# A two-layer encoder on one core: weight splitting moved from ScalarE and VectorE to GpSimd transfers that cast and add

## The chip, the core and the metric

One core of a Trainium2 chip runs the whole program. The metric is the device time of one execution in microseconds (us), and lower is better. The engines have short names in what follows: PE (TensorE, the matmuls; PEld is its weight load), DVE (VectorE), ACT (ScalarE), POOL (GpSimd) and SP (SyncE, which here only issues transfers). Each engine works through its own instruction queue in order, and an instruction whose semaphore isn't there yet holds up everything behind it on that engine.

## The reference, cut to what matters

512 tokens of 1024 channels pass through two layers and a final RMSNorm. In each layer one projection of the normalised input feeds three branches: (A) differential attention with four heads, (B) a retention with four heads, (C) a pooling mixer. Each branch is gated, and one output projection adds the result to the residual stream.

```python
h = rmsnorm(x, norm_w)
proj = jnp.einsum('bsd,de->bse', h, w_in)            # 1024 -> 4608 columns
aq, ak, av, ag, bq, bk, bv, bg, cu, cg = jnp.split(proj, splits, axis=-1)
...
mixed = jnp.concatenate([o_a, o_b, o_c], axis=-1)    # 1536 columns
return x + jnp.einsum('bse,ed->bsd', mixed, w_out)
```

All data are float32.

## The kernel before, in words

**Split products.** TensorE multiplies in a rounded float32 (`F32R`). So every operand is kept as two parts, a rounded one and what the rounding left over, and a product is three matmuls (`mm3`, line 499): high by high, high by low, low by high.

**Granules.** The weights stream through the core in 97 granules of 512 KB: 128 partitions by 1024 float32. A granule is used by 24 matmuls of 512 columns. `emit_granule` (line 428) makes a granule in three steps: a transfer on SP's queue into `wraw` (two buffers), a rounding copy on ACT into `wh`, and a subtraction on DVE into `wl` (`split`, line 453). `wh` and `wl` have five slots each (`WBUFS`, line 25). A granule's slot comes free when PE has read the granule that is five places ahead of it. As `wraw` is separate from these slots, the transfer can run up to two granules ahead of the free slot, and only the copy and the subtraction come after it.

**Units.** A layer is a list of named units (`ORDERS`, line 32). `bv` and `av` (`values`, line 694) take four granules at once and pass over four token tiles with them; a gate, `cu`, `cg` or half of a `qk` takes one granule (`proj_T`, line 515). Output units begin with `o` (`out_half`, line 557) and take one to four. The last unit, `oPQRS1`, takes four. `take` (line 443) emits granules until five past the current position exist. Layer 0 begins with `first_values` (line 702), which runs granules 0 to 3 against the transposed input as both arrive; `START` (line 27) is its order.

**Order.** The program is recorded first and then ordered by a list scheduler (`schedule`, line 201), which gives each engine its fixed order from estimated durations (`cost`, line 304). What the scheduler believes is not what the chip does: where an instruction is late on the chip, its engine's queue waits.

**Other users of the queues.** On SP's queue lie also the loads of x, the tables, and in `headnorm` (line 538) two small transfers that bring a row of statistics to all partitions. On POOL's queue lie the power operations of `headnorm` and `square` (lines 549 and 473), some clears in `c_pool` (line 905), and at the very end three products (line 989).

[...]

Of the kernel before, what the change touches and what calls it, by code (L numbers as in the profile page):

```python
# [9 lines left out]
F32 = mybir.dt.float32  # L10
# [19 lines left out]
# Order in which the units of a layer are recorded. An output unit is named by the pairs of 128-row blocks of w_out that it takes  # L30
# (A: P Q, B: R S, C: T U) and its half of the columns.
# [4 lines left out]
ORDERS = [o.split() for o in ORDERS]  # L36
PAIRS = {"P": ("A", 0), "Q": ("A", 2), "R": ("B", 0), "S": ("B", 2), "T": ("C", 0), "U": ("C", 2)}

# how far the units of a kind are moved ahead
# [4 lines left out]
# The kernel body is recorded first, on tiles that have no place yet. A list scheduler then fixes the order in which  # L44
# every engine issues its instructions and the slot each tile takes, and the program is emitted in that order.
# [17 lines left out]
class View:  # L63
    """Part of a recorded tile: partitions p0..p1, free offsets idx, and the steps that lead to it."""
# [32 lines left out]
    def window(self, row, first, pattern):  # L97
        """DRAM only: elements of a row from first on, by an access pattern of its own."""
        return View(self.base, self.p0, self.p1, self.idx, self.steps + (("window", row, first, pattern),))

    def spread(self, n):
        """Every element n times, along a new last axis."""
        return View(self.base, self.p0, self.p1, np.repeat(self.idx[..., None], n, -1), self.steps + (("spread", n),))
# [47 lines left out]
class Recorder:  # L151
# [9 lines left out]
    def add(self, name, engine, method, args, kw):  # L161
# [4 lines left out]
        ins = [v for v in list(args[1:]) + [x for k, x in kw.items() if k != "accum_out"] if isinstance(v, View)]  # L166
# [34 lines left out]
    def schedule(self):  # L201
# [39 lines left out]
        def ready(op):  # L241
            """A PSUM bank serves one engine at a time."""
# [55 lines left out]
WARM = 16  # matmuls on zeros at the start  # L298
QUEUE = 8  # transfers under way in a queue
FINE = 2  # weight granules of the first columns that come in two parts  # L300
# [3 lines left out]
def cost(engine, method, args, kw):  # L304
    """What an instruction weighs for the list scheduler: until its result stands, and on its engine."""
# [3 lines left out]
    if engine == "PE":  # L309
# [6 lines left out]
        return t, t  # L316
    if engine == "SP":
# [33 lines left out]
def record(ins: dict, out: bass.AP):  # L351
    nc = Recorder()
    x_d = ins["x"][0]
    w_in, w_out = ins["w_in"], ins["w_out"]
# [46 lines left out]
    def g_cols(l, c):  # L401
        return [w_in[l, :, c:c + P].rearrange("(k p) c -> p k c", p=P)]

    def g_tok(l, c):
        return [w_in[l, g * 256:(g + 1) * 256, c:c + 512].rearrange("(k p) c -> p k c", p=P) for g in range(4)]

    def g_out(l, e0, half):
        return w_out[l, e0:e0 + 256, HALF[half]].rearrange("(k p) c -> p k c", p=P)

    def unit_granules(l, u):  # L410
        if u in ("bv", "av"):
            return g_tok(l, BV if u == "bv" else AV)
        kind, i = u[:-1], int(u[-1])
        if kind in ("bg", "ag", "cu", "cg"):
            return g_cols(l, {"bg": BG, "ag": AG, "cu": CU, "cg": CG}[kind] + i * P)
        if kind == "bqk":
            return g_cols(l, BQ + i * P) + g_cols(l, BK + i * P)
        if kind == "qk":
            return g_cols(l, AQ + i * P) + g_cols(l, AK + i * P)
        if kind[0] == "o":  # L420
            return [g_out(l, "PQRSTU".index(c) * 256, i) for c in kind[1:]]
        return []

    granules = [g for l in range(DEPTH) for u in ORDERS[l] for g in unit_granules(l, u)]
# [3 lines left out]
    def emit_granule(parts=1):  # L428
        src = granules[len(wt)]
        shp = [P, src.shape[1], src.shape[2]]  # L430
# [28 lines left out]
    def square(t, half, junk, part=None):  # L459
        """Mean square of token tile t: the share of one half of its columns, or of a quarter in the second half."""  # L460
# [14 lines left out]
    def scaled(t, wb, dst, half):  # L475
        """One half of the columns of the rmsnorm of token tile t."""
        c = HALF[half]
        nc.vector.scalar_tensor_tensor(dst[:, c], xt[t][half], stats[t][:, 2:3], wb[:, c], op0=ALU.mult, op1=ALU.mult)

    def transpose4(src, step=None):  # L480
        """Four 128-column blocks of src, each transposed, in one bank."""
# [22 lines left out]
    def mm_stacked(ps, qk, m, cols):  # L504
        """Full product of slot m's query columns with its keys: both query parts lie stacked on partitions."""
# [16 lines left out]
    def stack_halves(dst, slots, src, scale, dup):  # L522
        """Split the 64 rows of each half of src. Without dup the low part goes to the other partition half of
        the same slot; with dup both parts take a slot each, present on both partition halves."""
# [13 lines left out]
    def headnorm(ov, scale, g):  # L538
        """ov * scale * rsqrt(mean over partitions of ov^2 + eps) * g"""
# [17 lines left out]
    def out_half(ms, half, after=None, before_end=None):  # L557
        """before_end: the last token tile comes in two quarters of the columns, and this follows the first."""
# [555 lines left out]
```

## Time and profile before

| | us |
|---|---|
| median of 2 runs (lowest, highest) | 682.1 (682.0, 682.2) |
| span of the profiled execution, first to last instruction | 679.9 |
[...]
| busy: PE, DVE, ACT, POOL | 659.5, 500.7, 353.9, 30.3 |
| weight granules: number, mean ACT copy, mean DVE subtraction | 97, 1.04, 1.21 |
| bytes moved by SP's queue, share of the 16 transfer engines | 71.29 MB, 36.3% |

How to read it: a busy PE isn't PE at full speed, because a matmul's end is modelled and neighbours overlap. The distance between the starts of two matmuls in a dense stretch is the true price. A wait is put down to what came last before it by the profile.

### The profile page before, as it was taken

To read this page: it belongs to the slowest core of one execution; us is meant where nothing else is said; L and a number is where in the kernel's file an instruction comes from. 1 tells how busy PE (TensorE), PEld (TensorE's weight loads), DVE (VectorE), ACT (ScalarE), POOL (GpSimd) and SP (SyncE) were. 2 spreads that over 40 slices of the span, in tenths; PEclk is the share of its full clock that TensorE was granted. 3 is DMA by queue.
4 is the path that set the end of the run, shared out by engine and by line. 5 is a ranking of instruction groups with operands and counts; after the bars stand their busy time and mean duration, and the time that the engine had idled before them with its cause. 6 is when DMAs were issued, how large, how long until landed. Compare 5 with 4: busy or idle time off the path is not lost.

```text
span 679.9 us, 8912 instructions
## 1 busy us (share of the span) xinstructions
PE 659.5 (97%) x3171; PEld 541.1 (80%) x3171; DVE 500.7 (74%) x954; ACT 353.9 (52%) x701; POOL 30.3 (4%) x51
## 2 busy tenths in 40 slices
PE   9969999999999999999999999899999999999996
PEld 7757887878788888887888888688888887888785
DVE  5468987787787998976574779767568957887733
ACT  7525673434376866553443756344447765655321
POOL 0000000000000000001010000000000000000011
PEclk9979999999999999999999999999999999999999
DMA  9447444323326223243322423532342143224302
GB/s 325 147 127 186 139 115 117 110 94 78 90 50 181 77 91 105 69 115 91 115 63 78 139 64 88 131 118 71 95 122 65 50 150 97 71 92 90 99 31 94
DMA packets 85141, 71.86 MB, mean 106 GB/s; under 512 B 6004, under 2 KB 67604, under 8 KB 85096
## 3 DMA queue, kind: packets, MB, share of 16 engines
q1 hardware_dynamic: 85096, 71.29, 36.3%
q8 instruction: 25, 0.41, 0.2%
q14 instruction: 20, 0.16, 0.1%
HBM read 69.09 MB, written 2.18 MB: 105 GB/s over the span
## 4 chain that ended last, share of the span: by engine, by line
PE 78%; DMA 10%; DVE 6%; issue 2%; ACT 2%; SPq 1%; POOL 0%; POOLq 0%; DVEq 0%; ACTq 0%
PE pj L1051 64%; PE lg L1051 6%; PE ov L1051 4%; PE tp L1051 4%; DMA hn<-row 3%; DMA wide<-dd 2%; DVE qk L1051 1%; DMA row<-edge 1%; DVE soft L1051 1%; DMA wraw<-in_w_in 1%; DVE wl L1051 1%; DMA cols<-in_scales 1%; DMA T<-in_xT_w 1%; DMA x<-in_x 1%; ACT soft L1051 1%
## 5 line engine op out<-in xcount | busy, mean ns | idle before, releaser
L1051 PE MATMUL pj<-hh,wh 128*128 128x512 f32 x448 | 178.5, 400 | 7.9 <-ACT wh L1051 6.5
L1051 PE MATMUL pj<-hl,wh 128*128 128x512 f32 x448 | 177.5, 397 | 0.0
L1051 PE MATMUL pj<-hh,wl 128*128 128x512 f32 x448 | 176.9, 396 | 0.0
L1051 ACT CAST wh<-wraw 128x1024 fp32r<-128x1024 f32 (+1 forms) x97 | 100.8, 1039 | 106.9 <-PE pj L1051 75.8
L1051 DVE TENSOR_TENSOR wl<-wraw,wh 128x1024 fp32r<-128x1024 f32 (+1 forms) x97 | 117.3, 1210 | 29.7 <-ACT wh L1051 29.1
L1051 PEld LDWEIGHTS pj<-hh,wh 128*128 128x128 f32 x448 | 84.7, 189 | 27.1 <-ACT wh L1051 7.0
L1051 PEld LDWEIGHTS pj<-hh,wl 128*128 128x128 f32 x448 | 84.6, 189 | 18.6
L1051 PEld LDWEIGHTS pj<-hl,wh 128*128 128x128 f32 x448 | 84.7, 189 | 17.7
L1051 PE MATMUL pj<-wh,mAC 128*128 128x512 f32 (+1 forms) x264 | 87.5, 391 | 0.0
L1051 ACT ACTIVATE soft<-soft,sm 128x512 f32<-128x512 f32 x96 | 67.8, 718 | 33.9 <-DVE sm L1051 33.5
L1051 DVE TENSOR_TENSOR x<-x,pj 128x512 f32<-128x512 f32 (+1 forms) x65 | 43.6, 675 | 23.2 <-PE pj L1051 22.8
L1051 PEld LDWEIGHTS pj<-wh,mAC 128*128 128x128 f32 x264 | 49.0, 188 | 10.3
L1051 PE MATMUL lg<-qk 128*128 128x512 f32 (+1 forms) x192 | 51.4, 361 | 1.5 <-DVE soft L1051 1.5
L1051 PE MATMUL pj<-wl,mAC 128*128 128x512 f32 (+1 forms) x132 | 51.4, 389 | 0.0
L1051 POOL TENSOR_TENSOR st<-st,neghalf 128x4 f32<-128x4 f32 (+1 forms) x28 | 25.1, 896 | 477.3 <-DVE st L1051 379.2
L1051 DVE CUSTOM_DVE_ANT_0 soft<-lg,wide 128x512 f32<-128x512 f32 x64 | 43.3, 687 | 1.9 <-PE lg L1051 0.3
L1051 PE MATMUL pj<-wh,mB 128*128 128x512 f32 (+1 forms) x136 | 44.5, 383 | 0.0
L1051 PE MATMUL pj<-wh,hl 128*128 128x512 f32 x104 | 41.4, 398 | 0.0
L1051 PE MATMUL pj<-wh,hh 128*128 128x512 f32 x104 | 41.3, 398 | 0.0
L1051 PE MATMUL pj<-wl,hh 128*128 128x512 f32 x104 | 41.2, 396 | 0.0
L1051 PEld LDWEIGHTS lg<-qk 128*128 128x128 f32 x192 | 32.5, 188 | 9.6 <-DVE soft L1051 2.5
L1051 PE MATMUL ov<-T,vh 128*128 128x256 f32 x192 | 39.1, 284 | 0.4 <-DVE og L1051 0.3
(151 smaller groups left out, 949.7 us busy)
## 6 DMA issues: line engine op xcount, KB each, us to landing
wraw<-in_w_in SPq DMA_DIRECT2D x71, 512.0 KB, 4.6
wraw<-in_w_out SPq DMA_DIRECT2D x24, 512.0 KB, 4.1
hn<-row SPq DMA_DIRECT2D x16, 256.0 KB, 3.9
wide<-gd SPq DMA_DIRECT2D x8, 448.0 KB, 4.0
T<-in_xT_w SPq DMA_DIRECT2D x8, 258.0 KB, 4.1
x<-in_x SPq DMA_DIRECT2D x8, 256.0 KB, 5.0
wide<-dd SPq DMA_DIRECT2D x8, 256.0 KB, 4.8
out<-T SPq DMA_DIRECT2D x8, 256.0 KB, 2.1
```

Of the source, the lines that this page charges most:

```text
L1051: op.inst = getattr(getattr(tc.nc, name), method)(*[real(a) for a in op.args], **{k: real(v) for k, v in op.kw.items()})
```

## The change

Host side: all weights are laid out anew as an array `wg` with one row block per granule, [granule][128][1024], so that a partition's share of a granule is 4 KB in one piece. `w_in` and `w_out` are no longer inputs. The list of granules is the same, in the same order.

Granules 0 to 3 are made as before, only from `wg`. Each of the other 93 is made by

1. a transfer on POOL's queue from `wg` (float32) into `wh` (`F32R`), which rounds if the transfer casts,
2. ACT: `wl` = -`wh`,
3. a second transfer on POOL's queue that adds the same granule of `wg` onto `wl`.

`wraw` has no part in them. With the last granule goes a guard: 512 of its high columns are rounded once more on ACT, the difference is formed on DVE, and a million times the difference is added to the residual tile `x[0][0]`. The scheduler's `cost` gets an entry for transfers on POOL, and the recorder learns that an accumulating transfer reads its target.

```diff
+        at, (nk, nc_) = granules[len(wt)]
+        shp = [P, nk, nc_]
+        src = ins["wg"][at].rearrange("p (k c) -> p k c", k=nk)
+        if len(wt) >= 4:
+
+            hi = sb("wh", shp, WBUFS, F32R)
+            lo = sb("wl", shp, WBUFS, F32R)
+            nc.gpsimd.dma_start(hi, src)
+            nc.scalar.activation(lo, hi.bitcast(F32), AF.Copy, scale=-1.0)
+            nc.gpsimd.dma_start(lo, src, accum_op=ALU.add)
+            wt.append((hi, lo))
+            if len(wt) == len(granules):
+                again, left = sb("soft", [P, S], 4, F32R), soft()
+                nc.scalar.copy(again, hi[:, 0, :].bitcast(F32))
+                nc.vector.tensor_tensor(left, hi[:, 0, :].bitcast(F32), again.bitcast(F32), op=ALU.subtract)
+                nc.vector.scalar_tensor_tensor(xt[0][0], left, 1e6, xt[0][0], op0=ALU.mult, op1=ALU.add)
+            return
         raw = sb("wraw", shp, 2)
...
+    if engine == "POOL" and method == "dma_start":
+        return 5500, 1500
...
+        kw_ins = [args[0]] if "accum_op" in kw else []
...
+    wg = np.empty((len(weight_granules()), P, 1024), np.float32)
+    for g, (name, l, (r, c), (nk, n)) in zip(wg, weight_granules()):
+        g[:] = np.asarray(inputs[name])[l, r:r + nk * P, c:c + n].reshape(nk, P, n).transpose(1, 0, 2).reshape(P, 1024)
+    a["wg"] = wg
```

## Rows read from the trace of the kernel before

**Rows 1.** The page: span and busy time of each engine.

```profile
span 679.9 us, 8912 instructions
...
PE 659.5 (97%) x3171; PEld 541.1 (80%) x3171; DVE 500.7 (74%) x954; ACT 353.9 (52%) x701; POOL 30.3 (4%) x51
```

**Rows 2.** Groups by line, op and tile: count, busy us, mean ns, idle before.

```profile
L1051 DVE TENSOR_TENSOR wl<-wraw,wh 128x1024 fp32r<-128x1024 f32 (+1 forms) x97 | 117.3, 1210 | 29.7 <-ACT wh L1051 29.1
L1051 ACT CAST wh<-wraw 128x1024 fp32r<-128x1024 f32 (+1 forms) x97 | 100.8, 1039 | 106.9 <-PE pj L1051 75.8 <-DMA wraw<-in_w_in 28.9 <-issue 1.8
...
L1051 DVE TENSOR_TENSOR qk<-soft,qk 64x512 fp32r<-64x512 f32 x32 | 21.9, 685 | 3.1 <-ACT qk L1051 2.4
...
L1051 DVE CAST qk<-qk 64x1024 fp32r<-64x1024 f32 x24 | 16.5, 689 | 0.7
...
L1051 POOL TENSOR_TENSOR soft<-x,T 128x512 f32<-128x512 f32 x3 | 3.9, 1302 | 19.9 <-DVE x L1051 13.5 <-issue 6.4
```

**Rows 3.** The chain that ended last, a dense stretch: start us, us, what.

```profile
352.06 37.49 PE pj L1051 x161
```

**Rows 4.** Windows of the start: length, busy us of PE, PEld, DVE, ACT, POOL; clock, transfer share, GB/s.

```profile
10.00:20.00 10.00, 10.00 (x45) 8.13 (x44) 6.76 (x13) 7.63 (x15) 1.11 (x2) 1.00 1.05 390
...
27.00:33.00 6.00, 6.00 (x28) 4.83 (x27) 2.50 (x8) 2.39 (x5) 0.00 (x0) 1.00 0.00 0
33.00:40.00 7.00, 0.79 (x4) 0.32 (x2) 2.30 (x5) 0.77 (x1) 0.00 (x0) 0.76 0.35 112
40.00:50.00 10.00, 9.67 (x36) 7.81 (x37) 8.31 (x26) 3.63 (x5) 0.00 (x0) 0.83 0.46 131
```

**Rows 5.** Waits of SP's queue: for whom, us in total, times, longest.

```profile
SPq L1051 <- DVE wl L1051: 302.6, 77, 17.0
...
SPq L1051 <- DMA row<-edge: 7.8, 1, 7.8
```

**Rows 6.** Timeline of the start, SP: start us, us, what.

```profile
23.95 0.38 SPq L1051 DMA_DIRECT2D row<-edge  x1
32.24 0.34 SPq L1051 DMA_DIRECT2D rb<-row  x1
32.69 9.25 SPq L1051 DMA_DIRECT2D wraw<-in_w_in  x3
```

**Rows 7.** Timeline of the start, PE and DVE around the stop.

```profile
37.70 0.69 DVE L1051 TENSOR_TENSOR cos<-cos,rb 128x512 f32<-128x512 f32 x1 [7.48 <-DMA rb<-row]
...
40.33 0.80 PE L1051 MATMUL pj<-hh,wh 128*128 128x512 f32 x1 [6.54 <-ACT wh L1051]
```

**Rows 8.** Transfers into wraw, time from issue to landing.

```profile
DMA to landing us min/median/max: 2.9/4.3/6.5
```

**Rows 9.** Timeline of ACT's copies: the start, layer 1's first values, the end.

```profile
28.36 1.04 ACT L1051 CAST wh<-wraw 128x1024 fp32r<-128x1024 f32 x1
...
363.51 1.05 ACT L1051 CAST wh<-wraw 128x1024 fp32r<-128x1024 f32 x1 [0.85 <-PE pj L1051]
...
640.44 1.05 ACT L1051 CAST wh<-wraw 128x1024 fp32r<-128x1024 f32 x1 [4.28 <-PE pj L1051]
...
650.18 1.05 ACT L1051 CAST wh<-wraw 128x1024 fp32r<-128x1024 f32 x1
```

**Rows 10.** Timeline: last matmul of layer 1's first values; first evictions of the last unit.

```profile
366.98 0.40 PE L1051 MATMUL pj<-wl,hh 128*128 128x512 f32 x1
...
657.14 0.69 DVE L1051 TENSOR_TENSOR x<-x,pj 128x512 f32<-128x512 f32 x1 [3.11 <-PE pj L1051]
```

**Rows 11.** Two windows in which PE stood still in mid-run (columns as in rows 4).

```profile
100.00:120.00 20.00, 18.38 (x101) 15.48 (x100) 15.87 (x25) 7.98 (x13) 0.00 (x0) 1.00 0.47 120
...
420.00:440.00 20.00, 17.52 (x94) 14.05 (x92) 16.31 (x26) 9.85 (x22) 1.02 (x1) 1.00 0.46 97
```

**Rows 12.** Waits of ACT: for whom, us in total, times, longest.

```profile
ACT wh L1051 <- PE pj L1051: 75.8, 39, 7.4
```

**Rows 13.** The chain: the power operation of one headnorm (columns as in rows 3).

```profile
298.51 1.02 POOL st L1051
```

More of the change, by code (lines that the diff above doesn't have):

```diff
@@ L36, with weight_granules @@
 ORDERS = [o.split() for o in ORDERS]
+def weight_granules():
+    out = []
+    for l in range(DEPTH):
+        for u in ORDERS[l]:
+            if u in ("bv", "av"):
+                out += [("w_in", l, (256 * g, BV if u == "bv" else AV), (2, 512)) for g in range(4)]
+                continue
+            kind, i = u[:-1], int(u[-1])
+            if kind in ("bg", "ag", "cu", "cg"):
+                out.append(("w_in", l, (0, {"bg": BG, "ag": AG, "cu": CU, "cg": CG}[kind] + i * P), (8, P)))
+            elif kind in ("bqk", "qk"):
+                out += [("w_in", l, (0, c + i * P), (8, P)) for c in ((BQ, BK) if kind == "bqk" else (AQ, AK))]
+            elif kind[0] == "o":
+                out += [("w_out", l, ("PQRSTU".index(c) * 256, 512 * i), (2, 512)) for c in kind[1:]]
+    return out
 PAIRS = {"P": ("A", 0), "Q": ("A", 2), "R": ("B", 0), "S": ("B", 2), "T": ("C", 0), "U": ("C", 2)}
@@ L165, in add @@
         outs = [args[0]] + ([kw["accum_out"]] if "accum_out" in kw else [])
-        ins = [v for v in list(args[1:]) + [x for k, x in kw.items() if k != "accum_out"] if isinstance(v, View)]
+        kw_ins = [args[0]] if "accum_op" in kw else []
+        ins = [v for v in list(args[1:]) + [x for k, x in kw.items() if k != "accum_out"] + kw_ins if isinstance(v, View)]
         deps, bases = {}, []
@@ L353, in record @@
     x_d = ins["x"][0]
-    w_in, w_out = ins["w_in"], ins["w_out"]
     def sb(tag, shape, bufs=1, dt=F32, name=None):
@@ L398, in record @@
     ident = sb("ident", [P, P])
[L401 to L424, printed above, removed]
+    granules = [(i, shape) for i, (_, _, _, shape) in enumerate(weight_granules())]
     wt = []
@@ L428, in emit_granule @@
     def emit_granule(parts=1):
-        src = granules[len(wt)]
-        shp = [P, src.shape[1], src.shape[2]]
+        at, (nk, nc_) = granules[len(wt)]
[14 more added lines that the diff above has]
+            return
         raw = sb("wraw", shp, 2)
@@ L1089, in _arrays @@
 def _arrays(inputs):
-    plain = ("x", "norm_w", "w_in", "diff_lambda", "pool_w", "w_out", "rel_bias", "final_norm_w")
+    plain = ("x", "norm_w", "diff_lambda", "pool_w", "rel_bias", "final_norm_w")
     a = {n: np.ascontiguousarray(inputs[n]) for n in plain}
```

## The prediction

> **What bounds the kernel now.** I read the page's busy times first: PE is busy for 659.5 of 679.9 us, DVE for 74%, ACT for 52%, POOL for 4% [rows 1]. A busy PE may still be slow, so the next view is the chain of waits, for the true price of a matmul: a stretch without a gap has 161 matmuls in 37.49 us, 0.233 us each [rows 3]. A granule feeds 24 matmuls, 5.6 us, and 97 granules make 543 us. The kernel is bound by PE, and a change beside PE can win only PE's standstill, some 20 us of the span. It can lose far more, because weights that come late stop PE at once.
>
> Where PE stands still is read from the windows. From 33 to 40 us it worked 0.79 of 7 us [rows 4]. The timeline shows how that ends: PE starts again at 40.33 after 6.54 us of idleness, when a `wh` copy is done [rows 7]. That copy waited for its transfer, and the timeline of SP shows why the transfer was late: it lay in SP's queue behind `rb<-row`, which needed the row issued at 23.95 and went out at 32.24; only at 32.69 came the weights [rows 5, 6]. DVE, too, sat 7.48 us in front of `cos`, for the same `rb` [rows 7], with a weight subtraction queued behind it. Afterwards the granted clock is down to 0.83, and PE starts 36 matmuls in the 10 us from 40 to 50 [rows 4] where 43 would fit at 0.233 us. The other two standstills that matter are 1.6 us and 2.5 us in mid-run [rows 11], both while DVE is loaded to about 80%. The rest lies ahead of the first weights and behind the last matmul, and the change doesn't touch it.
>
> **The change, part by part.**
>
> *Removed from DVE:* 93 subtractions of 1.21 us [rows 2], 113 us of its 501. DVE isn't the bound, so this counts only where PE waits for it: at most the 4.1 us of the two mid-run windows [rows 11]. I take half, -2.0 (from 0 to -4.1).
>
> *Removed from SP:* 93 transfers. SP waited 302.6 us for subtractions to free `wraw` [rows 5], with rows and tables queued behind; I count this with the 2.0.
>
> *ACT:* a copy of 1.04 us becomes a negation of the same size; I take 1.04, so nothing. The copies waited 75.8 us for PE to free a slot [rows 12]; now POOL has that wait, and ACT waits for the first transfer instead.
>
> *Added to POOL:* 186 transfers. No row shows the issue of one by POOL. Bounds: SP's issue of 0.38 us [rows 6] below, POOL's 1.30 us for an operation on 128x512 [rows 2] as the nearest row on that engine. I take 1.3: 242 us, 36% of POOL. What lies behind them are the power operations of each headnorm and norm, and their rows follow them on the way back to PE [rows 13]. POOL's queue also stops at its head, on a slot as ACT did (up to 7.4 us [rows 12]) or on ACT's negation. Four headnorms lie on the chain; four issues of 1.3 are 5.2 us, partly covered by other matmuls. I take +2.0 (0 to four waits of 7.4, 30).
>
> *The start.* Granules 4 to 8 no longer stand behind `rb<-row` on SP nor behind `cos` on DVE. PE could go on through three product banks from 33 to 44 us, and `rb` was there at 37.7 [rows 7]. Gain: 6.5 us of idleness and 7 matmuls of 0.233 (1.6 us) that the low clock cost, -8.1. Against it stands traffic: from 10 to 20 us the transfer engines are full at 390 GB/s [rows 4], where 512 KB take 1.34 us, and about one and a half granules more now move in that time. +2.0. (Ends: 0 if `rb` or the weights come that much later, -8.1 if the traffic is hidden.)
>
> *The way of a granule.* Before, the raw data lay ready when a slot came free, and copy and subtraction took 1.04 + 1.21 = 2.3 us. Now both transfers come after the slot. Call the time from free slot to finished `wl` C. The first transfer: issue 1.3 and landing 4.3 (median; 2.9 to 6.5 [rows 8]). The negation: 1.04 and about 1.0 in ACT's queue (ACT is busy half the time; up to the longest wait, 7.4). The second transfer: issue 1.3, and a landing that no row shows. It reads its target too, so below stands the 2.9 of a plain one and above twice the longest, 13. I take 6.5, the longest plain one, because the bytes read double while the fixed part of the landing doesn't. C = 1.3 + 4.3 + 1.0 + 1.04 + 1.3 + 6.5 = 15.4 us (8 to 30 with all ends together).
>
> With five slots, PE works on four other granules while one is filled, 4 x 5.6 = 22.4 us. C of 15.4 is hidden there. It isn't hidden where four granules are used together and come free almost at once:
>
> - *Layer 1's first values.* A slot came free just before 363.5 [rows 9], and the last matmul of the unit starts at 366.98 [rows 10]. One granule is already there, 24 matmuls, so PE lasts to 367.2 + 5.6 = 372.8. The next one stands at 363.4 + 15.4 = 378.8: +6.0 (0 at C of 9.4 or less). Layer 0's first values run over the granules one after another, and both `av` units are woven into attention heads, whose matmuls cover the gap; I cost these at nothing. Without that cover each `av` would cost the same 6.0.
> - *The last unit.* Its fourth granule got its slot just before 650.2 [rows 9], and PE needs it 1.4 us before the end of the first tile (evicted at 657.14 [rows 10]), at 655.7. It now stands at 665.6. PE can work on the other three granules for three tiles in three banks, 54 matmuls from 651.5, 12.6 us, to 664.1: +1.5.
>
> *The guard* is one ACT copy and two DVE operations in front of a DVE that stands idle for 3.1 us there [rows 10]: 0. If it stopped DVE until that granule's first transfer lands (650.2 + 1.3 + 4.3 = 655.8), the eviction at 657.14 would still be in time.
>
> *Sum:* 679.9 - 2.0 + 2.0 - 8.1 + 2.0 + 6.0 + 1.5 = 681.3 us of span. The median stands 2.2 above the span now, so 683.5.
>
> [...]
>
> **The rivals.**
>
> *R1, weights too late.* C comes near or above 22.4 us. Then every dense stretch stops PE once in each granule. At C = 26 the cycle of five slots is (26 + 5.6)/5 = 6.3 us a granule against 5.6; over about half of the 93 granules that is 33 us, with 16.6 at layer 1's first values and 12.1 at the end: 683.5 - 7.5 + 61.7 = 738; at C = 21 the dense stretches still hold, and 11.2 and 7.1 make 694. For it: the second landing is unknown, and POOL's and ACT's queues each stop at their heads. Against it: C must be half as long again as my sum. It decides above C of 22.
>
> *R2, POOL or the transfers can't keep pace.* On average a granule is wanted every (650.18 - 28.36)/91 = 6.8 us [rows 9], in dense stretches every 5.6. POOL falls behind from 2.8 us an issue, the engines if the adding transfer occupies them for more than 5.6 - 1.34 = 4.3 us, over three times a copy. At 8 us for both transfers: 92 x 8 = 736, with 28 us ahead and 24 behind, 788 us of span, 790 as a median. [...]
>
> *R3, faster by over 2%.* All gains and no loss: 679.9 - 8.1 - 4.1 + 2.2 = 670. It needs C under 9.4 and free traffic, and even so hardly reaches 668.5, since PE's matmuls alone leave so little.
>
> *R4, the transfer only copies.* Then `wh` isn't rounded and the guard shows it in the output. Its instructions and bytes are the same, so its time is that of the case it falls in.
>
> **How the numbers follow.** Forecast (C between 8 and 19, pace kept): 0.53, with its own range 672 to 697. R1: 0.18. R2: 0.19. R3: 0.08, mostly just short of 2%. Something else: 0.02. Two per cent, 13.6 us, is about what a measurement of this kernel can tell from no change. Within 2%, to 695.7: the forecast without its slow end (0.50) and most of R3 (0.05), 0.55. Slower by over 2%: R1, R2 and that end, 0.40. Faster by over 2%: 0.05. The range reaches down to R3's 670 and up through R1's 738, and leaves out R2 and little more.
>
> **What the profile would show.** The start: PE works through from 33 to 40 us and the granted clock stays at 1. Layer 1's first values: PE idle for some 6 us behind them, waiting for `wl` from a transfer. Dense stretches: no PE wait on `wh` or `wl`; if there is one in each granule, R1 or R2 holds, and the gap between issue and landing tells them apart: long landings with an idle POOL are R1 or full engines, a POOL busy to over 80% is R2. DVE: 93 subtractions gone and about 390 us busy. POOL's power operations: where they start more than 2 us after their inputs, the +2.0 was too small. The forecast is wrong if POOL's issues cost more than 2.8 us, or if the adding transfer lands after more than 11 us.

## The result and the profile after

The changed kernel takes 755.3 us (754.4 to 756.1) against 682.1 before: a ratio of 1.107, 95% interval 1.103 to 1.111. It is 73 us slower, above the forecast (683.5) and above its whole range (670 to 738).

The page of after, which answers to [rows 1], with two DMA queues added. q0 carries the transfers that POOL issues, q1 those of SP:

```profile
span 754.3 us, 8990 instructions
...
PE 682.7 (91%) x3171; PEld 553.2 (73%) x3171; DVE 406.7 (54%) x864; ACT 354.9 (47%) x702; POOL 163.1 (22%) x235
...
q0 software_dynamic: 26496, 96.48, 58.5%
q1 hardware_dynamic: 16680, 23.05, 11.2%
```

DVE has lost 94 us of work, as planned, and nothing came of it. PE stands still for 71.6 us of the span, before for 20.4. The line to stop at is q0: POOL's transfers hold the 16 engines for 58.5% of the span, 441 us, or 4.8 us for each of 92 granules. (92 is right, and all of them are in the trace. The text ahead of the prediction counts 97 granules and 93 moved ones, but 97 is the number of copies: the list in the kernel has 96 granules, and one of the first four comes in two parts.) Before, SP's transfers, nearly all that there were, held them for 36.3%.

Where PE stood still, by the waits of PE (for whom, us in total, times, longest):

```profile
PE tp L1064 <- ACT hn L1064: 12.8, 4, 6.0
PE pj L1064 <- DVE soft L1064: 7.6, 1, 7.6
PE pj L1064 <- DMA wl<-in_wg: 6.4, 6, 1.7
PE pj L1064 <- DVE u L1064: 5.7, 1, 5.7
PE tp L1064 <- DVE soft L1064: 5.2, 3, 2.8
...
PE tp L1064 <- DMA soft<-dd: 4.9, 1, 4.9
```

Only 6.4 us are direct waits for a weight that POOL brings. Most of the others are waits for headnorms (`hn`), for the products with `rb` (`soft`, `u`), for a table (`dd`); one of 5.1 us, not shown, is for a softmax column, and what stands behind it stays open. Worked out from the starts of neighbouring matmuls in the trace, against the usual distance for their kind: gaps longer by over 1.5 us hold 10.0 us before and 57.1 after, shorter ones 5.7 and 16.9, and matmuls that are up to 0.2 us late, such as those at a granted clock of 0.50 behind a stop, 9.7 and 24.5. The differences, 47.1, 11.2 and 14.8 us, make the 73.

Traced back through the waits of the other engines, the waits for `hn`, for the products with `rb` and for `dd` end at a transfer on SP's queue. (The longest of the three for `tp<-DVE soft`, 2.8 us, ends at ACT, which stood in front of a negation until a first transfer had landed, 9 us after its issue.) Issues with KB each and the median time to landing:

```profile
wh<-in_wg POOLq DMA_DIRECT2D x92, 512.0 KB, 5.0
wl<-in_wg POOLq DMA_DIRECT2D x92, 512.0 KB, 6.8
hn<-row SPq DMA_DIRECT2D x16, 256.0 KB, 5.7
...
x<-in_x SPq DMA_DIRECT2D x8, 256.0 KB, 7.7
...
rb<-row SPq DMA_DIRECT2D x1, 256.0 KB, 8.3
...
row<-edge SPq DMA_DIRECT2D x1, 2.0 KB, 9.3
```

Before, `hn` landed after 3.9 us, `x` after 5.0, `rb` after 5.4, and SP waited 7.8 us for `row<-edge` [rows 5]. (The two medians for `hn` rest on the 6 and 4 of its 16 transfers for which the view gives a landing. By the semaphore updates with which the transfers report their end, all 16 counted, they are 4.2 and 5.1. `row<-edge` takes 8.3 to 11.5 us in kernels without the change as well, so its 9.3 is no sign of load.) A headnorm's row makes two steps, a store to DRAM (`row<-st`) and the load of `hn`, and the store is later by as much: median 1.9 us before and 3.1 after, over all 16. SP's waits for it, in the kernel before:

```profile
SPq L1051 <- DMA row<-st: 14.0, 10, 2.8
```

and in the changed one:

```profile
SPq L1064 <- DMA row<-st: 49.1, 16, 6.1
```

VectorE's wait for `hn` has grown with them. Before:

```profile
DVE og L1051 <- DMA hn<-row: 17.4, 10, 5.6
```

The waits of POOL, ACT and DVE in the changed kernel:

```profile
POOL wl L1064 <- ACT wl L1064: 200.1, 63, 8.6
...
ACT wl L1064 <- DMA wh<-in_wg: 50.8, 23, 8.1
DVE og L1064 <- DMA hn<-row: 49.3, 11, 8.8
```

The longest of PE's waits for `hn`, 6.0 us, ends at 702.56, and the chain that leads there has both steps (start us, us, what):

```profile
688.62 5.81 DMA row<-st
...
694.49 6.48 DMA hn<-row
```

The start, in the windows (columns as in [rows 4]); the last one answers to [rows 11]:

```profile
20.00:40.00 20.00, 19.02 (x80) 14.99 (x81) 9.39 (x28) 12.74 (x24) 4.64 (x7) 1.00 1.00 299
40.00:60.00 20.00, 11.71 (x45) 8.63 (x43) 6.71 (x28) 1.62 (x2) 2.88 (x4) 0.82 0.70 118
60.00:80.00 20.00, 10.07 (x30) 7.51 (x31) 7.36 (x14) 5.16 (x6) 3.40 (x8) 0.58 0.66 129
420.00:440.00 20.00, 17.11 (x73) 13.29 (x72) 3.19 (x5) 7.46 (x10) 5.24 (x7) 1.00 0.93 197
```

and the kernel before, in the third of them:

```profile
60.00:80.00 20.00, 20.00 (x90) 16.01 (x89) 16.34 (x22) 14.62 (x21) 0.06 (x2) 1.00 0.59 163
```

Until 40 us PE does better than before. Then it starts 45 and 30 matmuls in windows of 20 us where the kernel before started 79 and 90, and the granted clock is down to 0.82 and 0.58 of full speed. These are means: in windows of 1 us it is 1.00 from 30 to 52 us, 0.50 from 53 to 76 and 1.00 again from 77. Over the whole span it is 0.956, before 0.994. The timeline says why (start us, us, what, and the idle time before it), to be read beside [rows 6, 7]:

```profile
36.98 0.37 SPq L1064 DMA_DIRECT2D row<-edge  x1
46.33 0.34 SPq L1064 DMA_DIRECT2D rb<-row  x1
...
54.75 0.69 DVE L1064 TENSOR_TENSOR cos<-cos,rb 128x512 f32<-128x512 f32 x1 [12.67 <-DMA rb<-row]
...
56.81 0.63 ACT L1064 ACTIVATE gate<-soft 128x512 f32<-128x512 f32 x1 [15.81 <-DVE soft L1064]
...
61.78 1.04 ACT L1064 ACTIVATE wl<-wh 128x1024 fp32r<-128x1024 f32 x1
...
63.25 0.87 POOL L1064 DMA_DIRECT2D wl<-in_wg  x1 [18.93 <-DVE hn L1064]
...
56.83 0.80 PE L1064 MATMUL pj<-hh,wh 128*128 128x512 f32 x1 [7.62 <-DVE soft L1064]
```

`row<-edge` goes out 13 us later than before because `x` came late (ACT's last square on it starts at 34.54, before at 22.16), it takes 9.3 us, and `rb` lands at 54.7 in place of 37.7. Of these 17 us, then, 13 come from the late `x`. Four queues show what follows. DVE stands in front of `cos` for 12.7 us, and PE starts again at 56.83 after 7.6. ACT stands in front of `gate`, which needs a product with `rb`; behind `gate` in its queue lie an operation on a table, for which it waits 3.4 us more, and then a negation, done at 62.8. POOL stands 18.9 us in front of the transfer that adds to it. (The row names DVE's `hn`. The next such transfer, at 65.09, follows its negation by the same 0.4 us, so it was the negation.)

### The profile page after: what moved, and what is told of

Read it like the earlier page. It is cut to its first block, busy times and chain, and to the rows that moved or that the text cites. A ratio compares the mean times of both kernels' runs of the same rounds, so it can differ in the third digit from the quotient of the medians.

```text
span 754.3 us, 8990 instructions
## 1 busy us (share of the span) xinstructions
PE 682.7 (91%) x3171; PEld 553.2 (73%) x3171; DVE 406.7 (54%) x864; ACT 354.9 (47%) x702; POOL 163.1 (22%) x235
## 3 DMA queue, kind: packets, MB, share of 16 engines
q0 software_dynamic: 26496, 96.48, 58.5%
q1 hardware_dynamic: 16680, 23.05, 11.2%
## 4 chain that ended last, share of the span: by engine, by line
PE 44%; DMA 23%; issue 18%; POOL 6%; DVE 5%; ACT 3%; SPq 0%; POOLq 0%; DVEq 0%; ACTq 0%
PE pj L1064 37%; DMA hn<-row 5%; DMA row<-st 4%; PE lg L1064 4%; DMA wh<-in_wg 4%; POOL wl L1064 3%; DMA wl<-in_wg 2%; PE tp L1064 2%; POOL wh L1064 2%; DMA sin<-in_c_sin 2%; POOL st L1064 2%; PE ov L1064 1%; DMA wraw<-in_pool_w 1%; DVE soft L1064 1%; DMA row<-edge 1%
## 5 line engine op out<-in xcount | busy, mean ns | idle before, releaser
L1064 PE MATMUL pj<-hh,wh 128*128 128x512 f32 x448 | 181.1, 405 | 15.2 <-DVE soft L1064 7.6
L1064 PE MATMUL pj<-hh,wl 128*128 128x512 f32 x448 | 180.4, 405 | 4.7 <-DMA wl<-in_wg 4.7
L1064 PE MATMUL pj<-hl,wh 128*128 128x512 f32 x448 | 180.1, 403 | 0.0
L1064 POOL DMA_DIRECT2D wl<-in_wg x92 | 82.6, 898 | 231.4 <-ACT wl L1064 200.1
L1064 ACT ACTIVATE wl<-wh 128x1024 fp32r<-128x1024 f32 x92 | 96.7, 1056 | 53.3 <-DMA wh<-in_wg 50.8
L1064 PEld LDWEIGHTS pj<-hh,wh 128*128 128x128 f32 x448 | 86.5, 193 | 36.0 <-DVE soft L1064 8.3
L1064 POOL DMA_DIRECT2D wh<-in_wg x92 | 54.8, 595 | 251.0 <-PE pj L1064 248.4
L1064 PE MATMUL pj<-wh,mAC 128*128 128x512 f32 (+1 forms) x264 | 90.3, 405 | 3.7 <-ACT mAC L1064 3.0
L1064 DVE TENSOR_TENSOR x<-x,pj 128x512 f32<-128x512 f32 (+1 forms) x65 | 43.8, 675 | 37.8 <-PE pj L1064 37.6
L1064 PEld LDWEIGHTS pj<-wh,mAC 128*128 128x128 f32 x264 | 51.2, 197 | 15.6 <-ACT mAC L1064 3.4
L1064 PE MATMUL pj<-wl,mAC 128*128 128x512 f32 (+1 forms) x132 | 53.6, 406 | 0.0
```

Of the source, the lines that this page charges most:

```text
L1064: op.inst = getattr(getattr(tc.nc, name), method)(*[real(a) for a in op.args], **{k: real(v) for k, v in op.kw.items()})
```

## Experiments

One execution each where no interval is given; those of the kernel before lay between 680 and 685 us beside them, so that 5 us are no difference. Four theories of the 73 us stood at the beginning, and their names return in the expectations: **traffic** (the engines are so loaded that other transfers land late), **way** (a granule takes longer than the other four cover), **heads** (what stands behind a waiting instruction on POOL or ACT is late), **order** (the planner's new order is worse). In the diffs, `+` and `-` are against the changed kernel.

### The two halves, the layout, and fewer bytes

The layout alone:

```
-        if len(wt) >= 4:
+        if len(wt) >= 1000:
```

> The changed kernel with all 97 granules on the old path (SP's transfer, ACT's copy, VectorE's subtraction), but still read from the packed array in rows of 4 KB. Four theories of the 73 us lost are under test. Traffic: the two transfers of POOL hold the transfer engines for 58.5% of the span, so everything else that is moved (rows, x, tables, headnorm rows) lands later, and the stages behind it stop TensorE. Way: from a free slot to a finished wl it takes longer than the 22.4 us that the other four granules cover. Heads: POOL's and ACT's queues stand with their first instruction on a slot or a transfer, and what is queued behind it (power operations, copies) is late. Order: the planner's order of the work became worse with the new instructions. All four expect this kernel near the one before, 675 to 685 us, because none of what they blame is in it. A time above 690 would say that the packed layout itself costs something; under 675, that it helps.

682.2 us, ratio 0.999 (0.997 to 1.002): the packed array costs and gives nothing. It is the base of the later kernels on the old path.

Only the first transfer:

```
+            raw = sb("wraw", shp, 2)
 ...
+            nc.sync.dma_start(raw, src)
             nc.gpsimd.dma_start(hi, src)
-            nc.scalar.activation(lo, hi.bitcast(F32), AF.Copy, scale=-1.0)
-            nc.gpsimd.dma_start(lo, src, accum_op=ALU.add)
+            nc.vector.tensor_tensor(lo, raw, hi.bitcast(F32), op=ALU.subtract)
```

> Half of the change: POOL's transfer rounds into wh, the raw granule comes by SP as before, and VectorE subtracts wh from it; no adding transfer, no negation. The bytes moved are the same as with both halves, but the second transfer is a plain one. Traffic: if rounding and adding cost the engines alike, about 2.4 us each where a plain one costs 1.3 to 1.4, this gives back a quarter of the excess, 720 to 745; if the adding one is the costly one, 685 to 710. Way: issue, landing of 5.0 and a subtraction of 1.2 us are some 8 us, well covered, 680 to 695. Heads: POOL has half of its instructions and no wait for ACT, ACT none for a transfer, 690 to 720. Order: 680 to 690.

699.6 us. q0 on its page:

```profile
q0 software_dynamic: 13248, 48.24, 21.8%
```

Only the second:

```
+            raw = sb("wraw", shp, 2)
 ...
-            nc.gpsimd.dma_start(hi, src)
+            nc.sync.dma_start(raw, src)
+            nc.scalar.copy(hi, raw)
             nc.scalar.activation(lo, hi.bitcast(F32), AF.Copy, scale=-1.0)
             nc.gpsimd.dma_start(lo, src, accum_op=ALU.add)
```

> The other half: the raw granule comes by SP, ACT rounds it into wh and negates that into wl, and only the adding transfer is POOL's; no subtraction on VectorE. Traffic: as for the other half, 720 to 745 if both kinds cost alike; 730 to 755 if the adding one is the costly one. Way: 1.0 + 1.0 + 0.9 + 6.8 us and queues make some 11 us, covered: 680 to 695. Heads: POOL waits for ACT as before but not for slots, ACT has one more copy but waits for early transfers only, 695 to 725. Order: 685 to 695.

733.1 us. q0:

```profile
q0 software_dynamic: 13248, 48.24, 37.8%
```

The same number of packets and bytes on both pages, and not the same load: 21.8% of 697.8 us over 92 transfers is 1.65 us each, 37.8% of 731.3 is 3.0. The packets say it too: one of 4 KB takes 159 ns (median) when SP only copies it, 174 when it is rounded, 328 when it is added. By these medians rounding in flight is nearly free, and adding costs the engines twice a copy. The halves cost 17 and 51 us; each of them still carries SP's raw granules, which the whole change doesn't. An adding packet took 1.89 times as long as a rounding one (328 against 174 ns). That it reads its target too was my reason for a longer landing; no run here shows whether that read is what takes the time.

All instructions and waits, an eighth of the bytes:

```
+            fh, fl, fs = (v.rearrange("p k c -> p (k c)") for v in (hi, lo, src))
+            nc.vector.memset(fh[:, P:].bitcast(F32), 0.0)
-            nc.gpsimd.dma_start(hi, src)
+            nc.gpsimd.dma_start(fh[:, 0:P], fs[:, 0:P])
 ...
-            nc.gpsimd.dma_start(lo, src, accum_op=ALU.add)
+            nc.gpsimd.dma_start(fl[:, 0:P], fs[:, 0:P], accum_op=ALU.add)
```

> The changed kernel, but both transfers of POOL move only the first 128 of 1024 columns of each granule (an eighth of the bytes; VectorE fills the rest of wh with zeros, ACT's negation the rest of wl, so seven eighths of each weight granule are left out). All instructions, waits and slots stay. Traffic: the stolen time goes with the bytes, 685 to 700 us, and x, rb, row and hn land as before the change (4 to 5, 5.4, 3.1 and 3.9 us). Way: the landings of 5.0 and 6.8 us shrink by the part that the bytes make, at most some 2 us each, so the way falls from about 17 to 13 us or more; if the way is what stops TensorE, 690 to 720. Heads: POOL still waits 200 us and more for slots and for ACT, so at least 730. Order: no change, 745 to 755.

708.7 us: 46.6 of the 73 come back. q0 and the landings, columns as above:

```profile
q0 software_dynamic: 26496, 12.07, 12.2%
...
wh<-in_wg POOLq DMA_DIRECT2D x92, 64.0 KB, 2.2
wl<-in_wg POOLq DMA_DIRECT2D x92, 64.0 KB, 2.7
hn<-row SPq DMA_DIRECT2D x16, 256.0 KB, 3.8
...
rb<-row SPq DMA_DIRECT2D x1, 256.0 KB, 3.8
```

`hn` and `rb` land no later than before the change, and so VectorE's wait for the headnorms' rows, 49.3 us in the changed kernel, is small again:

```profile
DVE og L1066 <- DMA hn<-row: 10.3, 8, 2.4
```

The landings of POOL's own transfers fell as well, so this run alone doesn't tell traffic from way. About 26 us stay.

### Traffic, way or heads

Traffic that nobody waits for, beside the old path. The first form of it (878.4 us) missed its purpose: the planner put the transfers far ahead of their granules, and they filled the engines until 507 us.

```
 (old path for all granules)
+            nc.gpsimd.tensor_copy(mark, hi[:, 0, 0:1].bitcast(F32))
+            spare = nc.tile("dram", "spare", [P, 1040], 4, F32R)[:, 0:1024]
+            nc.gpsimd.dma_start(spare, ins["wg"][at])
+            nc.gpsimd.dma_start(spare, ins["wg"][at], accum_op=ALU.add)
```

> The old path for all granules (as with the packed layout alone, 682.2 us), and beside it, for each granule from the fifth on, the two transfers of POOL with their bytes (one rounding, one adding), into spare DRAM that nobody reads; POOL issues them when the granule's wh has been rounded. So the traffic is there and nothing waits for it. Traffic (what is lost is lost because rows, x, rb and headnorm rows land later): 46 of the 73 us came back when the bytes were taken away, so 715 to 735. Way and heads: only POOL's power operations stand behind the new issues, 682 to 692. If transfers into DRAM hold the engines for less than those into SBUF (1.65 and 3.0 us), the traffic theory's figure falls in that proportion.

The second form puts both transfers behind `mark` in the planner's order too:

```
+                nc.ops[-1].deps.append(m)
```

> As the last kernel with free traffic, but paced: there the planner had put POOL's transfers ahead of the granules they belong to, so they ran as fast as the engines allowed and filled them until 507 us. Here the two transfers into spare DRAM stand in POOL's order behind the copy that waits for the granule's own wh. Nothing waits for them. Traffic: 46 of the 73 us came back when the bytes were taken away, and DRAM targets cost the engines about as much as SBUF ones (4.42 against 4.65 us a granule), while SP's raw transfers, 1.4 us a granule, come on top: 720 to 750. Heads and way: 682 to 692.

809.6 us, 127 more than without these transfers, where 40 to 70 were expected. q0, and the landing of SP's raw granules (3.9 us with the layout alone):

```profile
q0 software_dynamic: 26496, 96.48, 51.9%
...
wraw<-in_wg SPq DMA_DIRECT2D x95, 512.0 KB, 7.1
```

Transfers whose data nobody uses cost more here than the whole change did. The size was missed because SP's raw granules now land late as well, and `wh` with them: ACT waits 81.6 us for them in 29 times. A part may not be traffic: POOL waits 226 us for its own spare tiles to come free, and its power operations stand behind that. So the run shows the direction, and the size is only a bound.

A sixth slot:

```
-WBUFS = 5
+WBUFS = 6
 ...
-        raw = sb("wraw", shp, 2)
+        raw = sb("mB", shp, 4)
 (the one other tile that lay in wraw moves to T)
```

> The changed kernel with six slots for weights in place of five (the first four raw granules lie in tiles that layer 0 doesn't use yet, so the memory is there). Transfers, bytes and instructions stay; a granule gets 5.6 us more of cover. Way: the waits for wl and all that follows from them go, 690 to 720. Traffic: the lateness of rows and tables stays, 740 to 755. Heads: POOL's heads wait as long as before in sum, but for slots further ahead, so what stands behind them is late as before: 735 to 755.

755.0 us, no difference. The headnorms' rows are as late:

```profile
DVE og L1064 <- DMA hn<-row: 45.7, 12, 8.0
```

So it isn't too few slots for the way of a granule. The second transfer copying in place of adding:

```
-            nc.gpsimd.dma_start(lo, src, accum_op=ALU.add)
+            nc.gpsimd.dma_start(lo, src)
```

> The changed kernel with the second transfer copying (and rounding) instead of adding, behind the same negation, so the low part of the weights is left out; instructions, order and waits stay. By the halves run alone, an adding transfer holds the engines for 3.0 us and a rounding one for 1.65, so the load falls from 4.65 to 3.3 us a granule. Traffic: about 45 us belong to 4.65 us a granule; with 3.3, 715 to 735. Way: the second landing falls from 6.8 to about 5.0 us, 1.8 of some 17 us, so at least 740. Heads: at least 740.

722.9 us, 32 less:

```profile
q0 software_dynamic: 26496, 96.48, 44.2%
```

44.2% of 721.0 us over 184 transfers is 1.73 us each. With order, instructions and bytes untouched, adding in place of copying is worth 32 of the 73 us. Two things go with it: the second transfer lands sooner (4.6 us for 6.8), and its issue on POOL is shorter (mean 0.56 us for 0.90). The sixth slot says that the first is worth little; the next run bears on the second.

POOL left to its transfers:

```
-            nc.gpsimd.tensor_tensor(st[:, 2:3], st[:, 1:2], neghalf[:, 0:1], op=ALU.pow)
+            nc.vector.tensor_scalar(st[:, 2:3], st[:, 1:2], 0.0, 1.0, op0=ALU.mult, op1=ALU.add)
 ...
-            nc.gpsimd.memset(u[:, 0:PADL], 0.0)
+            nc.vector.memset(u[:, 0:PADL], 0.0)
 (the headnorms' power operation and the other border of u in the same way)
```

> The changed kernel with POOL left to its transfers (and the last three products): the clearing of u's borders goes to VectorE, and the power operations are replaced by a VectorE operation of the same tiles that writes 1.0, so the norms' factors are left out. Heads: what stood behind POOL's waits (u's borders at 63 us, the 28 power operations) comes in time, which is the part that taking the bytes away didn't give back, some 26 us: 720 to 735. Traffic and way: the transfers and slots are as before, 745 to 755, less at most 5 for the power operations' own time on the way of 16 headnorms.

748.9 us: 6.4 less, little above what one run can tell; the expectation had laid POOL's 18.9 us at the start to u's borders, and they were ACT's. What stands behind POOL's waits is a small part.

### The start and the plan

The first 12 granules on the old path:

```
-        if len(wt) >= 4:
+        if len(wt) >= 12:
```

> The changed kernel, but the first 12 granules keep the old path, so the start is that of the kernel before and POOL's transfers begin some 40 us later. The start of the changed kernel lost about 18 of the 73 us (309 matmuls by 80 us before, 220 after). Traffic that delays x and rb at the start is a part of the loss of its own: 735 to 742. If the same loss is only moved to where POOL's transfers begin: 750 to 756.

732.2 us: 23 us belong to the start, more than the 13 to 20 that the range expected.

The planner told what transfers take in the changed kernel:

```
     if engine == "POOL" and method == "dma_start":
-        return 5500, 1500
+        return (6800, 900) if "accum_op" in kw else (5000, 600)
 ...
                 op.end = bus + 908
+                to, of = (v.base.tag if isinstance(v, View) else "" for v in op.args[:2])
+                op.end += 7300 if (to, of) == ("row", "edge") else 5600 if to == "rb" else 2500
```

> The changed kernel whole; only the planner's costs are set to what the changed kernel's transfers took: first transfer 5.0 us (0.6 of POOL), second 6.8 (0.9), row<-edge 7.3 more than assumed, rb 5.6 more, every other transfer of SP 2.5 more. Bytes and instructions are the same. Stale plan (the order was laid out for transfers that land earlier, and TensorE stands where it meets them): most of the 73 us comes back, 690 to 715. Capacity (the transfers are slow by themselves and no order hides them): 735 to 755.

721.7 us with every byte and every instruction of the change: 33.5 us back, between the two expectations. POOL's transfers land as late as before this edit (5.3 and 6.9 us), SP's a little sooner (`rb` 6.4 for 8.3 us, `x` 5.4 for 7.7, `hn` over all 16 rows 4.5 for 5.1). So the new order moves the work that needs them further back, and it also moves the transfers themselves; this run doesn't part the two. Two of PE's waits, the longest in total and that for weights:

```profile
PE tp L1066 <- ACT hn L1066: 7.0, 6, 2.3
...
PE pj L1066 <- DMA wl<-in_wg: 3.2, 4, 1.2
```

Either way, nearly half of the loss goes with an order made for transfers that land earlier than they did. Both edits together, told costs and 12 granules on the old path:

> The planner told the measured landings (721.7 us alone) and the first 12 granules on the old path (732.2 us alone). The two edits gave back 33.5 and 23.0 us; were they independent, 698.7. If both mend the same thing at the start (with the told costs the matmuls by 100 us are 375 against 315 in the changed kernel, so part of the start is mended there already), 708 to 722. What is left above 682 is then what the engines' load costs with an order that fits it.

725.4 us, above both expectations and no better than the told costs alone: the two gains don't add. Not because the start was already whole. By 100 us this kernel has started 415 matmuls, with the told costs alone 371; by 600 us they stand at 2664 and 2665. The lead from the start is lost on the way, and why is open. (The told costs are those of the loaded engines, and with the old path the start isn't loaded so.)

Only the headnorms' rows late, and no traffic; the planner is kept from knowing:

```
 (old path for all granules; in the planner, the step out of hop ends when it starts)
-        nc.sync.dma_start(row.rearrange("(p j) -> p j", j=4), st[:, 4:8])
+        nc.sync.dma_start(hop.rearrange("(p j) -> p j", j=4), st[:, 4:8])
+        nc.sync.dma_start(row, hop)
```

> No part of the change: the old path for all granules, but each of the 16 headnorms' rows takes one more step through DRAM (2 KB from one row to another) that the planner is not told of, so hn comes some 2 to 4 us later without any traffic. In the changed kernel row and hn together come about 2 to 5 us later than before. If late headnorm rows alone are what stops TensorE in mid-run: 715 to 730 (some 50 us over 16 headnorms, 3 us each). If they are mostly covered: 684 to 695, and the loss needs the lateness of the weights and the other transfers as well.

700.9 us, 18.7 above the old path with the same layout, for a step that lands after 2.2 us, 16 times. DVE's wait, before 17.4 us:

```profile
DVE og L1067 <- DMA hn<-row: 30.2, 13, 4.4
```

Over half of 35 us of lateness reaches the end. This is less than the mid-run loss, but it needs no late weight at all.

### Two versions of the old path, and what remains

The same correction of the planner's costs without the change. First the start alone, then all transfers (the second edit has 900 in place of 0):

```
 (old path for all granules)
                 op.end = bus + 908
+                to, of = (v.base.tag if isinstance(v, View) else "" for v in op.args[:2])
+                op.end += 6000 if (to, of) == ("row", "edge") else 2700 if to == "rb" else 0
```

> No part of the change: the old path for all granules from the packed layout, with one correction in the planner's costs, that row<-edge lands 6.0 us and rb 2.7 us later than it had assumed (measured 7.8 and 5.4 us). The planner then puts weights ahead of rb in SP's order, and subtractions ahead of cos on VectorE. If the 6.5 us that TensorE stood still at 33.8 us, and the low clock behind it, were owed to that order, as the forecast's -8.1 had it: 672 to 677 us. If rb itself is the limit, the stall moves to the first product that needs it: 679 to 684.

679.4 us, ratio 0.996 (0.994 to 0.998). Weights now go out ahead of `rb`:

```profile
24.94 0.39 SPq L1066 DMA_DIRECT2D row<-edge  x1
26.63 5.38 SPq L1066 DMA_DIRECT2D wraw<-in_wg  x2
36.46 0.33 SPq L1066 DMA_DIRECT2D rb<-row  x1
```

and still the gain is 2.7 us: `row<-edge` takes 11.5 us, `rb` goes out at 36.46, and the stop moves to the first product that needs it (PE's longest wait is now 4.2 us, for `soft`).

> The same, with 0.9 us more for every other transfer of SP in the planner's costs (measured 4.4 us for a granule against 3.5 assumed, 3.9 against 2.7 for a headnorm's row). If the late rows of the headnorms were what stops TensorE in mid-run (some 4 us before the change), 668 to 676; if the new order only shifts work, 676 to 686.

671.5 us, ratio 0.984 (0.980 to 0.987): 1.6% faster than the kernel before, clear of the noise, though less than 2%. Span and busy time:

```profile
span 671.4 us, 8905 instructions
...
PE 657.8 (98%) x3171; PEld 540.4 (80%) x3171; DVE 501.1 (75%) x954; ACT 352.8 (53%) x701; POOL 30.2 (4%) x51
```

PE stands still for 13.6 us in place of 20.4.

What neither bytes nor start explain was looked for in three runs. The thin transfers with the start on the old path:

> The two edits that gave back most, together: the first 12 granules on the old path (732.2 us alone), and of the others only an eighth of the bytes moved (708.7 us alone; seven eighths of these weights are left out, VectorE fills wh with zeros). If start and traffic explain the loss between them, 683 to 692. If the queues' heads and the plan's new order hold a part of their own, what is left over stays: 700 to 709.

706.4 us, no less than the thin transfers alone (708.7) within what one run can tell, and so in the upper expectation: something besides start and traffic holds a part. With the start as changed, but a plan that fits the short landings:

> The changed kernel with an eighth of the bytes (708.7 us alone; seven eighths of these weights are left out, VectorE fills wh with zeros) and the planner told the landings that go with it: 2.2 and 2.7 us for POOL's transfers, row<-edge 7.3 more than assumed, rb 2.7 more, all others 0.9 more. The kernel with the old path and nearly the same told costs took 671.5. If the 24 to 26 us that bytes and start don't explain are a plan that doesn't fit, 672 to 688. If they are the queues' heads, and VectorE's fills of wh that only this kernel has, 695 to 709.

702.4 us, again in the upper expectation: 6 us less than the thin transfers alone, so a plan that fits is the smaller part of what remains. And with ACT's negation and POOL's small operations moved:

```
-            nc.scalar.activation(lo, hi.bitcast(F32), AF.Copy, scale=-1.0)
+            nc.gpsimd.tensor_scalar(lo, hi.bitcast(F32), -1.0, None, op0=ALU.mult)
 (thin transfers, told costs, and POOL's power operations and borders of u on VectorE, as in the kernels above)
```

> The last kernel with little traffic and a plan that fits it (702.4 us), and in addition no other work behind the waits of the two queues: the negation goes from ACT to POOL, so ACT no longer stands in front of it until the first transfer has landed (79.8 us in 34 waits), and POOL's small operations go to VectorE (u's borders; the power operations are replaced by a VectorE operation that writes 1.0, so the norms' factors are left out, as are seven eighths of the weights). If those two queues' heads are the remainder of some 30 us above the 671.5 of the old path with a fitting plan: 672 to 688. If it is VectorE's fills of wh, or anything else: 695 to 706.

732.0 us, outside both expectations, and so it tells nothing of the heads. POOL's negation took 2.85 us, and beside it DVE's product `og<-og,hn` took 843 ns in place of 679. First this kernel (groups: busy us, mean ns, idle before):

```profile
L1068 POOL TENSOR_SCALAR wl<-wh 128x1024 fp32r<-128x1024 f32 x92 | 261.2, 2847 | 167.5 <-DMA wh<-in_wg 108.2 <-DVE sm L1068 13.8 <-DVE wh L1068 10.3
...
L1068 DVE TENSOR_TENSOR og<-og,hn 128x512 f32<-128x512 f32 x16 | 13.5, 843 | 2.6 <-DMA hn<-row 2.6
```

and the one before it:

```profile
L1068 DVE TENSOR_TENSOR og<-og,hn 128x512 f32<-128x512 f32 x16 | 10.9, 679 | 4.0 <-DMA hn<-row 3.9
```

## Why the prediction was wrong, point by point

**The step that failed** is "Against it stands traffic ... +2.0". Traffic was priced as time that the engines need for one and a half granules at the start, and outside the start at nothing. Rival R2 asked only whether the engines keep pace with PE (under 4.3 us for the adding transfer, beside a copy). They do: the adding transfer holds them for 3.0 us, both for 4.65 to 4.8, and a granule is wanted every 5.6. But with the engines busy for 70% of the span, SP's transfers land later (`x` 7.7 us for 5.0, `rb` 8.3 for 5.4, a headnorm's store and load together some 2 to 3 us more), and what stands behind those was not in the sum. Taking the bytes away gives back 46.6 us, taking away only the adding 32. These two are shown, each by one run; that other transfers land later is read in the landings, and that late rows alone cost time is shown by the extra hop. The prediction's own signs of being wrong didn't see this coming: POOL's issues (medians 0.55 and 0.88 us, limit 2.8) and the adding transfer's landing (median 6.8 us, limit 11) both held, and yet the time lies beyond R1's 738.

**The order** stood nowhere in the forecast. It took the planner's order as given, though that order rests on landing times, and the change alters them. Told the true ones, the changed kernel takes 721.7. The two parts overlap (46.6 and 33.5 make more than the 73), so they can't be added. With plans made for measured landings on both sides it is 721.7 against 671.5: the change then costs some 50 us.

**The start, -8.1.** The mechanism was half right: PE works through from 33 to 40 us and the clock stays at 1. But `rb` moved from 37.7 to 54.7, which the bounds (0 to -8.1) didn't hold, and the start lost 23 us. Even without the change, weights ahead of `rb` are worth 2.7 us, since `rb` itself is next: by that run the term was three times too large.

**The way of a granule, 15.4 us.** The parts were off and the sum held: issue 0.6 and 0.9 us on POOL (1.3 taken), landing 5.0 and 6.8 (4.3 and 6.5 taken), and with the 1.0 of queue taken and ACT's 1.06 again 15.4. From a granule's first issue to its second landing the trace has a median of 14.9 us (10.5 to 32.7, four of 92 above 22.4). Parts that were off by 0.3 to 0.7 us cancelled; that the sum came out so close is luck. Five slots cover it, since a sixth gives nothing. The count of granules was off by one (92 in place of 93, 96 in place of 97), which makes the 543 us of matmuls 538 and changes no term of the sum. R1 didn't come about: PE waits 6.4 us for `wl` in all, 2.3 of them behind layer 1's first values, where I had put 6.0. No stop shows behind the last unit (+1.5 forecast). R2's pace held, and R3's gains came nowhere. (In R1, at C = 21, the first loss is 11.6 us and not 11.2.)

**POOL.** Its 184 issues are 137 us, not 242; the longest took 1.25 us where the median is 0.88, and no issue is longer than the median of its kind by over 0.4 us, with DVE busy for 54% of the span. POOL's heads cost 6.4 us (+2.0 taken, 0 to 30).

**DVE relief, -2.0.** The subtractions are gone, and nothing that could be seen came of it: in the two windows in which I had hoped for it, PE stood still for 1.6 and 2.5 us before and for 2.8 and 2.9 after. This is no like-for-like comparison, since the changed kernel is at other work by then (DVE is busy for 3.2 us of the second window, before for 16.3); the -2.0 itself was not measured.

**The guard, 0.** As forecast: DVE does its two operations from 729.83 on and then stands idle for 8.0 us.

```profile
739.25 0.69 DVE L1064 TENSOR_TENSOR x<-x,pj 128x512 f32<-128x512 f32 x1 [8.01 <-PE pj L1064]
```

**What stays open.** Thin transfers with a fitting plan still take 702.4 us against the 671.5 of the old path. The candidates are ACT's wait in front of the negation (79.8 us there), POOL's heads, and VectorE's fills of `wh`, which only the thin kernels have. The run meant to part them brought a cost of its own. Open, too, is where the kernel with both the told costs and the old start loses its lead.

## What to carry to other kernels

Before work is moved to transfers, add up how long they hold the transfer engines, in their own kind, and ask what else is on these engines and who waits for it; that they keep pace on average is not enough. Where an order was laid out for measured latencies, measure again after the change and lay it out anew before judging. Here the wrong landing times had cost the kernel before 1.6% as well.

## What the runs showed of the hardware that I had not expected

- A transfer that adds takes twice the engine time of one that copies (medians of 328 against 159 ns for a 4 KB packet), one that rounds hardly more (174). Nothing of it shows in bytes or packets.
- A store of 2 KB took 1.9 us (median of 16) beside engines held for 36% and 3.1 beside 70%, up to 6.5. It is the smallest transfer on the way of a headnorm, and it was late by as much as the 256 KB behind it. The store at the start, `row<-edge`, has 2 KB as well, but in 512 pieces of 4 bytes where the others have 128 of 16; it took 8.2 to 11.5 us with the change and without it.
- The share of the engines alone doesn't give the time. Share of q0 and q1 together, and time:

| kernel | share | us |
|---|---|---|
| thin | 24.0% | 708.7 |
| layout alone | 34.0% | 682.2 |
| rounding half | 56.0% | 699.6 |
| second transfer copies | 56.2% | 722.9 |
| changed kernel | 69.7% | 755.3 |
| adding half | 69.7% | 733.1 |
| changed, planner told | 72.8% | 721.7 |
| free traffic, paced | 80.2% | 809.6 |

- An operation of POOL on 128x1024 from SBUF took 2.85 us, and while POOL did 92 of them, DVE's `og<-og,hn` on 128x512, with both inputs in SBUF, went from 679 to 843 ns in the rows above. `x<-x,pj`, with one input in a product bank, stayed at 678 and 676, and so did `hn<-hn,u`, with both inputs in SBUF, at 692 and 693. Why some operations became slower no run here shows.
